# Double stores, VectorE and ScalarE programs without alignment, and a first load issued from ScalarE, in a batched matrix product on Trainium2

## Chip, cores, metric

One core of one Trainium2 chip. The metric is device microseconds of one execution; lower is better. Each kernel is run several times, and one execution has a profile. "Span" is the time from the first to the last instruction in the profile, which is some 1.8 us less than the device time of the same run.

## The reference

```python
# a: 16 x 512 (k) x 512 (m), b: 16 x 512 (n) x 512 (k), float32
def reference(a, b):
    return np.matmul(a.transpose(0, 2, 1), b.transpose(0, 2, 1)).astype(np.float32)
```

Per batch, 1 MB of a and 1 MB of b are read and 1 MB is written: 50.3 MB in all.

## The kernel before

Five engine programs run side by side, joined by semaphores. SyncE issues the loads and the last stores, ScalarE casts a to bf16, copies half of the result out of PSUM (where TensorE leaves its sums) and issues the other stores, VectorE casts b, moves the transposed b and copies the other half. TensorE transposes b and multiplies. The parts that matter here, with cuts marked:

```python
    LOADS = 4          # buffers of a and of b
    OUTS = 7           # result buffers, of one batch each
    LAG = 3
    FETCH = 128
    TAIL = 5           # stores issued by SyncE, at the end
    # ...
        def store(eng, j):
            eng.dma_start(out_v[j], o_sb[j % OUTS][:]).then_inc(
                o_out[j % OUTS] if j + OUTS < B else stored, 16
            )

        def run_sp(sp):
            for i in range(B):
                s, use = i % LOADS, i // LOADS
                if use:
                    sp.wait_ge(turned, i - LOADS + 1)
                sp.dma_start(b_sb[s][:], b_v[i]).then_inc(b_in[s], 16)
                if use:
                    sp.wait_ge(summed, MO * (i - LOADS) + 1)
                sp.dma_start(a_sb[s][:], a_v[i]).then_inc(a_in[s], 16)
            # ... the last five stores
    # ...
            dve.addr_align(FETCH, max_nops=0)      # head of VectorE's program
            cast_b(0)
            cast_b(1)
            turn(0)
            # ...
        def run_act(act):
            act.addr_align(FETCH, max_nops=0)      # head of ScalarE's program
            cast_a(act, 0, slice(None), 2)
            for i in range(B - 2):
                if i + 1 >= OUTS:
                    act.wait_ge(o_out[(i + 1) % OUTS], 16 * ((i + 1) // OUTS))
                cast_a(act, i + 1, slice(None), 2)
                copy_out(act, i, slice(2, 4), oa_go)
                if 0 <= i - LAG < B - TAIL:
                    store(act, i - LAG)
            # ...
```

Each `addr_align` leaves a branch in the trace, ScalarE's at 0.90 us (line 164) and VectorE's at 0.97 us (line 149).

## Time and profile before

| what | before |
|---|---|
| device time, median of 3 runs | 125.23 us (125.19 to 125.35) |
| span of the profiled run (it took 125.51 us) | 123.7 us |
| bytes moved, mean rate | 50.35 MB, 407 GB/s |
| busiest engine | TensorE, 69% of the span |
| two data queues together | 97.2% of 16 DMA engines' span |

The prediction shows and reads the lines for this. In short: DMA is full from the second slice to the last but one, no computing engine is, and the end waits for stores.

The prediction and all that follows use the packet records in the trace: start, duration, size and queue of each DMA packet. They carry no number of the DMA engine. I put them into 16 chains by time: in steady work each record starts 3 ns before the one ahead of it on its engine ends. Two chains of the same phase can be exchanged by this, so counts per chain are good to a few packets, while the ends of the 16 chains and the landings at the semaphores (16 for each transfer, 768 for the 48 transfers of the kernel before) are records themselves.

### The profile page before, as it was taken

Reading aid. Unit: us, or ns where it says so; the run is one execution under the profiler, and the core shown is the slowest. Engines: PE = TensorE matmul, PEld = TensorE weight load, DVE = VectorE, ACT = ScalarE, POOL = GpSimd, SP = SyncE. Lnnn points to the kernel's source line nnn. Section 1 sums busy time; section 2 is a strip of 40 time slices with the busy share of each in tenths; the row PEclk is TensorE's granted clock in tenths of the full one; section 3 lists DMA queues with packets and bytes.
Section 4 is the critical chain, followed back from the end, with each engine's and each line's share of the span. In section 5 each row is a group of like instructions: output and inputs, shape, how many; then the busy total and the mean of one; then the engine's idle time right before and its main releaser. Section 6 shows DMA issues by size and latency. Waiting matters only on the chain. (4 is left out here: it accounts for less than half of the span.)

```text
span 123.7 us, 1099 instructions
## 1 busy us (share of the span) xinstructions
PE 84.9 (69%) x392; PEld 48.2 (39%) x392; DVE 58.0 (47%) x50; ACT 45.9 (37%) x34; POOL 0.7 (1%) x6
## 2 busy tenths in 40 slices
PE   0042399949994997799499919919859965869600
PEld 0040155536462644455364602613535442524400
DVE  0032518455737755594653734716167370762200
ACT  0009410880466086317353080090906226034100
POOL 2000000000000000000000000000000000000000
PEclk9999999999999999999999995995899999599996
DMA  2999999999999999999999999999999999999992
GB/s 58 421 424 429 424 426 421 424 421 424 418 424 387 424 424 424 424 426 424 429 432 426 426 434 429 424 424 424 429 424 424 434 426 429 432 424 432 421 424 85
DMA packets 6914, 50.35 MB, mean 407 GB/s; under 512 B 768, under 2 KB 768, under 8 KB 768
## 3 DMA queue, kind: packets, MB, share of 16 engines
q1 hardware_dynamic: 5328, 38.80, 75.1%
q10 hardware_dynamic: 1584, 11.54, 22.1%
q14 instruction: 2, 0.02, 0.1%
HBM read 33.55 MB, written 16.78 MB: 407 GB/s over the span
## 5 line engine op out<-in xcount | busy, mean ns | idle before, releaser
L205 PE MATMUL o_ps<-bt_sb,a_bf 128*128 128x512 bf16 x256 | 67.5, 414 | 22.7 <-PEq L183 22.4
L205 PEld LDWEIGHTS o_ps<-bt_sb,a_bf 128*128 128x128 bf16 x256 | 28.5, 116 | 55.2 <-issue 33.8
L123 ACT CAST a_bf<-a_sb 128x2048 bf16<-128x2048 f32 (+1 forms) x16 | 29.6, 1847 | 33.8 <-DMA a_sb<-in_a_dram 33.8
L137 DVE CAST b_bf<-b_sb 128x2048 bf16<-128x2048 f32 x16 | 19.5, 1222 | 24.8 <-DMA b_sb<-in_b_dram 24.8
L132 DVE COPY o_sb<-o_ps 128x1024 f32<-128x1024 f32 (+1 forms) x17 | 19.7, 1160 | 20.3 <-PE o_ps L205 20.3
L193 PE MATMUL bt_ps<-identity,b_bf 128*128 128x128 f32 x136 | 21.0, 303 | 8.7 <-PEq L183 8.7
L132 ACT COPY o_sb<-o_ps 128x1024 f32<-128x1024 f32 (+1 forms) x17 | 16.3, 961 | 27.2 <-PE o_ps L205 27.2
L193 PEld LDWEIGHTS bt_ps<-identity,b_bf 128*128 128x128 f32 x136 | 20.3, 209 | 12.9 <-issue 10.9
L143 DVE COPY bt_sb<-bt_ps 128x1024 f32<-128x1024 f32 x16 | 19.5, 1221 | 11.6 <-PE bt_ps L193 11.6
L123 ACT ACT_TABLE_LOAD x1 | 1.3, 1283 | 9.1 <-DMA a_sb<-in_a_dram 9.1
L123 DVE CAST a_bf<-a_sb 128x1024 bf16<-128x1024 f32 x1 | 0.7, 694 | 0.5 <-DMA a_sb<-in_a_dram 0.5
L109 POOL TENSOR_SCALAR_AFFINE_SELECT identity<-identity 128x128 f32<-128x128 f32 x1 | 0.3, 292 | 0.2 <-POOL identity L107 0.2
L107 POOL MEMSET identity<- 128x128 f32 x1 | 0.2, 204 | 0.7 <-SPq L48 0.7
L249 POOL MEMSET const-bfloat16-1.0<- 128x1 bf16 x1 | 0.1, 101 | 0.0
L249 POOL MEMSET const-uint8-127<- 128x1 uint8 x1 | 0.1, 101 | 0.0
L249 POOL MEMSET const-float32-0.0<- 128x1 f32 x1 | 0.1, 98 | 0.2 <-issue 0.2
L249 POOL MEMSET const-float32-1.0<- 128x1 f32 x1 | 0.1, 98 | 0.0
## 6 DMA issues: line engine op xcount, KB each, us to landing
b_sb<-in_b_dram SPq DMA_DIRECT2D x16, 1024.0 KB, 16.5
a_sb<-in_a_dram SPq DMA_DIRECT2D x16, 1024.0 KB, 16.4
out_dram<-o_sb ACTq DMA_DIRECT2D x11, 1024.0 KB, 9.1
out_dram<-o_sb SPq DMA_DIRECT2D x5, 1024.0 KB, 8.4
```

The lines of the kernel that those rows point to most:

```text
L107: pool.memset(identity[:], 0.0).then_inc(id_go, 1)
L109: pool.affine_select(out=identity[:], in_=identity[:], compare_op=mybir.AluOpType.not_equal, fill=1.0, base=0, pattern=[[-1, P]], channel_ ...
L123: copy(a_bf[i % 2][:, part, :], a_sb[s][:, part, :]).then_inc(ac_go, n)
L132: copy(o_sb[i % OUTS][:, rm, :], o_ps[h][:, p, :]).then_inc(go, 1)
L137: dve.tensor_copy(b_bf[i % 2][:], b_sb[i % LOADS][:]).then_inc(bc_go, n)
L143: dve.tensor_copy(bt_sb[i % 2][:].rearrange("p j (ni no) -> p j ni no", no=NO), bt_ps[i % 2][:].rearrange("p j no ni -> p j ni no"),).then ...
L193: last = pe.transpose(bt_ps[x][:, j, no, :], w[:, no, j, :], identity[:])
L205: last = pe.matmul(o_ps[h][:, q, :], a_r[:, rk, 2 * h + q, :], bt_h[:, rk // 2, rk % 2, :], start=(rk == 0), stop=(rk == KO - 1),)
L249: nc = _bacc.Bacc("TRN2", target_bir_lowering=False, num_devices=1)
```

## The change

The intent: fewer transfers and fewer instructions on ScalarE, so that the programs of VectorE and ScalarE run without alignment and yet without an instruction packet in the span; and a start at which the first a is issued beside the first b.

```diff
-    OUTS = 7
+    OUTS = 5
     LAG = 3
-    FETCH = 128
-    TAIL = 5
+    TAIL = 3
+    H = B // 2
+    STORED = H - (H - OUTS) + 1
 ...
-        o_sb = [sb(f"o_sb{s}", [P, MO, N], f32) for s in range(OUTS)]
+        o_sb = [sb(f"o_sb{s}", [P, 2, MO, N], f32) for s in range(OUTS)]
 ...
-        def store(eng, j):
-            eng.dma_start(out_v[j], o_sb[j % OUTS][:]).then_inc(
-                o_out[j % OUTS] if j + OUTS < B else stored, 16
-            )
+        def store(eng, j, part=slice(0, 2)):
+            eng.dma_start(
+                out_v[2 * j + part.start:2 * j + part.stop].rearrange("b p mo n -> p b mo n"),
+                o_sb[j % OUTS][:, part],
+            ).then_inc(o_out[j % OUTS] if j + OUTS < H else stored, 16)
 ...   (SyncE)
-                sp.dma_start(a_sb[s][:], a_v[i]).then_inc(a_in[s], 16)
+                if i % 2 == 0 and i // 2 >= OUTS:
+                    sp.wait_ge(o_out[i // 2 % OUTS], 16 * (i // 2 // OUTS))
+                if i:
+                    sp.dma_start(a_sb[s][:], a_v[i]).then_inc(a_in[s], 16)
 ...   (SyncE's stores: two double ones, then batch 14 and batch 15 alone)
 ...   (VectorE: no alignment; its last two copies out as one; ScalarE's last two accordingly)
-            dve.addr_align(FETCH, max_nops=0)
-            copy_out(dve, B - 1, 0, last_go)
-            copy_out(dve, B - 1, 2, last_go)
+            copy_out(dve, B - 1, slice(0, 2), last_go)
 ...   (ScalarE: no alignment, no waits for result buffers, first load of a)
-            act.addr_align(FETCH, max_nops=0)
+            act.dma_start(a_sb[0][:], a_v[0]).then_inc(a_in[0], 16)
-                if i + 1 >= OUTS:
-                    act.wait_ge(o_out[(i + 1) % OUTS], 16 * ((i + 1) // OUTS))
-                if 0 <= i - LAG < B - TAIL:
-                    store(act, i - LAG)
+                j, odd = divmod(i - LAG, 2)
+                if odd and 0 <= j < H - TAIL:
+                    store(act, j)
```

More of the change, by code (lines that the diff above doesn't have):

```diff
@@ L92, in run_sp @@
                     sp.wait_ge(summed, MO * (i - LOADS) + 1)
-                sp.dma_start(a_sb[s][:], a_v[i]).then_inc(a_in[s], 16)
-            for j in range(B - TAIL, B):
-                if j + 1 < B:
-                    sp.wait_ge(summed, MO * (j + 1) + 3)
-                else:
-                    sp.wait_ge(last_go, MO)
-                store(sp, j)
-            sp.reg_mov(all_stored, 16 * OUTS)
+                if i % 2 == 0 and i // 2 >= OUTS:
+                    sp.wait_ge(o_out[i // 2 % OUTS], 16 * (i // 2 // OUTS))
+                if i:
+                    sp.dma_start(a_sb[s][:], a_v[i]).then_inc(a_in[s], 16)
+            for j in range(H - TAIL, H - 1):
+                sp.wait_ge(summed, MO * (2 * j + 2) + 3)
+                store(sp, j)
+            sp.wait_ge(summed, MO * (B - 1) + 3)
+            store(sp, H - 1, slice(0, 1))
+            sp.wait_ge(last_go, 3)
+            store(sp, H - 1, slice(1, 2))
+            sp.reg_mov(all_stored, 16 * STORED)
         def run_pool(pool):
@@ L131, in copy_out @@
             p = rm - 2 * h if isinstance(rm, int) else slice(None)
-            copy(o_sb[i % OUTS][:, rm, :], o_ps[h][:, p, :]).then_inc(go, 1)
+            copy(o_sb[i // 2 % OUTS][:, i % 2, rm, :], o_ps[h][:, p, :]).then_inc(go, 1)
         def run_dve(dve):
@@ L159, in run_dve @@
             cast_a(dve, B - 1, slice(KO // 2, KO), 1)
-            copy_out(dve, B - 1, 0, last_go)
-            copy_out(dve, B - 1, 2, last_go)
+            copy_out(dve, B - 1, slice(0, 2), last_go)
         def run_act(act):
-            act.addr_align(FETCH, max_nops=0)
+            act.dma_start(a_sb[0][:], a_v[0]).then_inc(a_in[0], 16)
             cast_a(act, 0, slice(None), 2)
             for i in range(B - 2):
-                if i + 1 >= OUTS:
-                    act.wait_ge(o_out[(i + 1) % OUTS], 16 * ((i + 1) // OUTS))
                 cast_a(act, i + 1, slice(None), 2)
                 copy_out(act, i, slice(2, 4), oa_go)
-                if 0 <= i - LAG < B - TAIL:
-                    store(act, i - LAG)
-            act.wait_ge(o_out[(B - 1) % OUTS], 16 * ((B - 1) // OUTS))
+                j, odd = divmod(i - LAG, 2)
+                if odd and 0 <= j < H - TAIL:
+                    store(act, j)
             cast_a(act, B - 1, slice(0, KO // 2), 1)
             copy_out(act, B - 2, slice(2, 4), oa_go)
-            copy_out(act, B - 1, 1, last_go)
+            copy_out(act, B - 1, 2, last_go)
             copy_out(act, B - 1, 3, last_go)
```

## The prediction

0.7 us for the instruction packets, 0.04 for semaphore packets and 0.05 for the first load make 0.8 (0.1 without the first), and at 0.7 to 0.3 that is 0.6 us.

> **What bounds the kernel now.** I looked first at the page's rows over time, then at its queues, then at sums over stretches of time, and last at what SyncE waits for at the end. On the page, DMA stands against every engine that computes:
>
> ```profile
> PE 84.9 (69%) x392; PEld 48.2 (39%) x392; DVE 58.0 (47%) x50; ACT 45.9 (37%) x34; POOL 0.7 (1%) x6
> ...
> DMA  2999999999999999999999999999999999999992
> GB/s 58 421 424 429 424 426 421 424 421 424 418 424 387 424 424 424 424 426 424 429 432 426 426 434 429 424 424 424 429 424 424 434 426 429 432 424 432 421 424 85
> ...
> q1 hardware_dynamic: 5328, 38.80, 75.1%
> q10 hardware_dynamic: 1584, 11.54, 22.1%
> q14 instruction: 2, 0.02, 0.1%
> ```
>
> No engine is busy over 69% of the span, while the DMA row is 9 from the second slice to the last but one, and the two data queues together took 75.1 + 22.1 = 97.2% of what 16 engines have. The windows (length, busy time by engine, clock, DMA share, GB/s) say the same by stage:
>
> ```profile
> 0.00:3.10 3.10, 0.00 (x0) 0.00 (x0) 0.00 (x0) 0.00 (x0) 0.70 (x6) 1.00 0.30 61
> 3.10:18.60 15.50, 6.18 (x21) 3.67 (x21) 4.20 (x4) 5.08 (x3) 0.00 (x0) 1.00 1.01 424
> 18.60:37.10 18.50, 16.67 (x85) 9.95 (x84) 11.27 (x10) 9.13 (x7) 0.00 (x0) 1.00 1.01 422
> 37.10:40.20 3.10, 1.39 (x8) 0.65 (x8) 2.36 (x2) 2.13 (x2) 0.00 (x0) 1.00 1.00 386
> 40.20:108.00 67.80, 53.66 (x250) 29.98 (x249) 36.84 (x31) 26.45 (x19) 0.00 (x0) 0.92 1.01 427
> 108.00:121.00 13.00, 6.99 (x36) 3.90 (x34) 3.30 (x4) 3.13 (x4) 0.00 (x0) 1.00 1.00 423
> ```
>
> Loads alone (3.1 to 37.1 us) run at 422 to 424 GB/s, loads mixed with stores at 427, stores alone (from 108 us) at 423. So the rate depends neither on direction nor on queue. TensorE is close to full only in 18.6 to 37.1 us (16.67 of 18.5 us) and still doesn't slow the DMA, as loads are queued ahead of it. The chain of waits on the page ends with PE at 116.4 us of 123.7, and is not the chain that matters; SyncE's own waits show that one (us in total, times, longest):
>
> ```profile
> SPq L260 <- DMA out_dram<-o_sb: 5.8, 1, 5.8
> ```
>
> SyncE sits 5.8 us at the end for stores that were all issued by 116.1 us. The bound is thus: start of the first transfer, plus bytes over a fixed rate, plus completion of the last.
>
> In the packet records this closes. There are 6,144 data packets of 8,192 bytes, 384 for each of 16 DMA engines; the usual record is 309 ns and the usual spacing from start to start 306 ns. 384 x 0.306 = 117.5 us. There are 768 four-byte packets (48 transfers x 16) of 9 ns, 48 an engine, which with the 3 ns overlap cost about 6 ns each, 0.3 us. The first data packet starts at 1.96 us, 1.0 us after SyncE began the first issue at 0.95; eight engines start by 2.04 us, the rest at 2.69 to 2.81, and first packets of up to 1.3 us make all reach their steady pace at about 3.1. A dip at 39.1 to 40.3 us, as the first store starts to move, costs about 0.3 us. The last packets then end at 120.97 to 121.49 us on fourteen engines, and at 121.97 and 122.21 on two. The last landing is at 122.68, the program's end at 123.7.
>
> [...]427 GB/s with both queues, 424 with one. [...]So a load of a on ScalarE's queue will share with the load of b rather than follow it. No first pair of loads in this trace shows that; stores do show it, as most 1 MB stores take 4.3 to 5.1 us from first to last packet beside loads, twice the 2.45 us a megabyte needs alone. [...]the trace has 9 ns records, so fewer transfers save little. [...]VectorE and ScalarE each take the branch that the alignment made, at 0.97 and 0.90 us, and two packets of q14 follow, at 1.93 us (1,356 ns) and 3.41 us (309 ns). Each has 8,192 bytes[...]. Whose they are the records don't say; I infer it from the times.
>
> **The change, part by part.**
>
> *Stores of two batches.* The bytes and the 8,192-byte pieces stay. ScalarE issues 5 stores, not 11, SyncE 4, not 5: 41 transfers instead of 48. Seven fewer semaphore packets an engine x 6 ns = 0.04 us saved. ScalarE saves 6 issues of 338 ns less the one it gains for a, some 1.7 us, and its waits for store buffers; all of that beside an engine 37% busy, so 0.
>
> *Could DMA run dry meanwhile?* The first store starts to be issued at 43.8 us, not 36.4. From the records, loads issued less data moved are lowest before the store, 2.1 MB (5 us of work) at 40 us; without the early store the same count gives 2.3 MB at 42.0, 2.1 at 45.0 and 1.85 at 48.6. The new wait is tighter: SyncE holds load a of batch 10 until the first double store has landed. Stores in this trace start to move some 3.5 us after the issue, so 47.5 us; 2 MB at half rate take 9.8 us; with landing some 57.9 us, against an issue at 51.4 now. By then 21 loads are issued, 22.1 MB moved, 2 of them stored: 0.9 MB left on SyncE's queue (2.1 us), while the second double store, issued at about 55.2, starts near 58.7. Close, not dry: 0. The later waits leave 2 MB and more. At the end six batches rather than five are issued from SyncE, the last load lands by my count near 105 rather than 110 us, and computing ends sooner, under stores that are queued anyway: 0.
>
> *Instruction blocks.* Without the alignment both engines run straight on; the built programs shrink from 74 to 67 instructions on ScalarE and from 64 to 62 on VectorE. [...]the two q14 packets go. Each displaced a data packet (309 ns) and upset the start of its DMA engine: a data record of 838 ns follows the second. Two packets and two late engines, 0.5 and 0.7 us behind the others: I take these for the same two. Then the last data packet ends at about 121.49 rather than 122.21: 0.7 us saved.
>
> *First load of a by ScalarE.* SyncE's second issue (starts 1.39 us, 0.43 us long) moves to ScalarE, free at about 0.9 to 1.0. DMA engines then already have 2.45 us of b to move, so an earlier a adds nothing; perhaps 0.05 us for an issue ahead of SyncE's. Interleaved, b lands near 9 us rather than 6.6. VectorE's first cast and PE's first transposes slip by up to 2.5 us, yet turning batch 0 waits behind the cast of b of batch 1 until 12.71 us even now, and 3 MB have moved by the same time either way. So the first product, at 14.4 us, should hardly move.
>
> Sum: 0.7 + 0.04 + 0.05 = 0.8 us if the fetches go, 0.1 if not. At 0.7 to 0.3 that is 0.6 us: 125.23 - 0.6 = 124.6.
>
> **The rivals.** *The fetch stays or moves*: [...]engines have slack and a packet costs a DMA engine 0.3 us, so the time stays at 125.1 or 125.2. *DMA runs dry at the new wait*: 0.9 MB is a thin margin and one slow stretch could cost 1 to 2 us, 125.5 to 126.5. Against it speaks that the store queue has 2 MB of its own at that time. *The start improves more*: two queues at once might bring the late eight engines (0.7 us behind) in at once; then 123.9. Against it: the early ones' first packets take so long that all are level at 3.1 us. *Fewer, larger stores move faster*: 427 GB/s mixed against 424 with loads alone leaves nothing to win, as packets have the same size.
>
> **Range and chances.** The middle is the weighted sum; 124.0 needs the fetch saving and a gain at the start, 125.5 a small loss at the new wait. 2% is 2.5 us: for a gain that long nothing is left between 97.2% and full, and a loss of that size takes a real stall. I give 1% to faster, 2% to slower.
>
> **What would show it right or wrong.** q14 gone from the queues, with both last engines ending within 0.6 us of the others, shows the fetch step right; q14 there with equal time, that it failed. A DMA row below 9, or GB/s under 380 near 55 to 62 us, shows the new wait to bite. First landings of a and b both near 9 us with PE's first product at 14.4 show the start right. The rate in stretches with stores should stay at 423 to 427 GB/s; over 430 would break the fixed-rate argument and with it the prediction.

## The result, and the profile after

The changed kernel took 125.43 us (median of 4 runs, 125.18 to 125.62), the kernel before 125.21 beside it (125.14 to 125.35). The ratio is 1.0015 with a 95% interval of 0.9992 to 1.0037. Neither the gain of 0.6 us came nor any other.

The page of the changed kernel, the rows over time and the queues:

```profile
DMA  3999999999999999999999999999999999999991
GB/s 72 395 432 435 430 424 419 424 416 419 422 416 419 424 424 424 424 435 432 427 432 424 427 424 424 424 424 432 424 435 427 424 432 429 430 424 422 424 424 69
...
q1 hardware_dynamic: 5296, 38.80, 74.9%
q10 hardware_dynamic: 1504, 11.53, 22.4%
```

DMA is as full as before, and the q14 line is gone: no instruction packet lies in the span. The same stretches as in the prediction (start:end, length, busy us of PE, PEld, DVE, ACT and POOL, clock, DMA share, GB/s):

```profile
3.10:18.60 15.50, 6.86 (x24) 4.35 (x25) 4.81 (x4) 5.08 (x3) 0.00 (x0) 1.00 1.00 422
18.60:37.10 18.50, 16.46 (x82) 9.46 (x80) 10.82 (x10) 9.56 (x8) 0.00 (x0) 1.00 1.01 422
37.10:40.20 3.10, 1.59 (x8) 0.84 (x9) 2.19 (x2) 1.70 (x1) 0.00 (x0) 1.00 1.01 418
40.20:108.00 67.80, 52.43 (x258) 29.98 (x256) 38.72 (x33) 27.04 (x20) 0.00 (x0) 0.97 1.01 426
108.00:121.00 13.00, 4.76 (x24) 2.86 (x24) 1.31 (x2) 2.52 (x4) 0.00 (x0) 0.89 1.01 427
```

The rates are those of before within 1%, except that the dip at 37 to 40 us (386 GB/s before) is absent. SyncE's waits:

```profile
SPq L98 <- DMA out_dram<-o_sb: 26.1, 3, 8.9
...
SPq L260 <- DMA out_dram<-o_sb: 8.5, 1, 8.5
```

The new wait for result buffers (L98) takes 26.1 us of SyncE in three waits, and DMA stays full through all of them. SyncE now waits 8.5 us for the end, as computing ends sooner, with the last stores queued longer. The start, from the timeline of the changed kernel (start, duration, instruction):

```profile
0.91 0.40 ACTq L168 DMA_DIRECT2D a_sb<-in_a_dram  x1
0.95 0.86 SPq L93 DMA_DIRECT2D b_sb<-in_b_dram  x2
1.86 0.42 SPq L100 DMA_DIRECT2D a_sb<-in_a_dram  x1
...
8.63 1.23 DVE L144 CAST b_bf<-b_sb 128x2048 bf16<-128x2048 f32 x1 [8.63 <-DMA b_sb<-in_b_dram]
...
13.69 3.58 PE L205 MATMUL o_ps<-bt_sb,a_bf 128*128 128x512 bf16 x8 [1.74 <-PEq L183]
```

In the timeline of the kernel before the same places read:

```profile
1.86 1.55 SPq L90 DMA_DIRECT2D b_sb<-in_b_dram  x1
...
6.60 1.23 DVE L137 CAST b_bf<-b_sb 128x2048 bf16<-128x2048 f32 x1 [6.60 <-DMA b_sb<-in_b_dram]
...
14.38 3.58 PE L205 MATMUL o_ps<-bt_sb,a_bf 128*128 128x512 bf16 x8 [4.45 <-PEq L183]
```

The first b comes 2.0 us later, since it shares with a, and the first product still starts 0.7 us earlier. SyncE's third issue took 1.55 us beside the instruction packet of before and takes 0.42 now.

Where then is the gain? The end of each of the 16 chains of packets, in us, shows it:

```
before   120.97 121.00 121.06 121.07 121.18 121.35 121.37 121.41 121.43 121.44 121.44 121.45 121.49 121.49 121.97 122.21
changed  120.92 120.93 120.97 120.97 120.98 120.99 121.00 121.01 121.02 121.18 121.19 121.21 121.24 121.26 121.26 122.08
```

Of the two late chains one is gone. Fifteen DMA engines are done by 121.26 us, a quarter of a microsecond sooner than the fourteen of before, and one still works until 122.08. (The missing dip would explain that quarter: 32 GB/s less over 3.1 us at 418 GB/s is 0.24 us, an estimate from the two windows that no run tests; e3, with slow packets near 46 us, has its fifteen done by 121.15.) In the windows, DMA share of 16 engines just before the end, before and then changed:

```profile
121.50:121.95 0.45, 0.00 (x0) 0.00 (x0) 0.00 (x0) 0.00 (x0) 0.00 (x0) 0.66 0.13 55
```

```profile
121.30:122.05 0.75, 0.00 (x0) 0.00 (x0) 0.00 (x0) 0.00 (x0) 0.00 (x0) 0.50 0.05 22
```

0.13 is two of 16 engines, 0.05 is one. The last engine decides: the last data packet moved by 0.12 us only (one profile of each kernel, and the spans of one kernel's runs differ by up to 0.5 us), the last landing from 122.68 to 122.55. The second part of the answer is not in the span at all: device time less span was 1.98 to 2.09 us in the four runs of the changed kernel, and is 1.73 to 1.83 in the 31 runs of the kernel before that were made beside the experiments. Together with the control c1 below, the mean span is 123.34 us over 9 runs of the changed kernel and 123.54 over those 31: 0.19 us gained in it, 0.25 lost outside.

### The profile page after: what moved, and what is told of

Its sections match the earlier page's. It is cut to its first block, busy times and chain, and to the rows that moved or that the text cites. A ratio compares the mean times of both kernels' runs of the same rounds, so it can differ in the third digit from the quotient of the medians.

```text
span 123.6 us, 1091 instructions
## 1 busy us (share of the span) xinstructions
PE 82.1 (66%) x392; PEld 47.5 (38%) x392; DVE 57.9 (47%) x49; ACT 45.9 (37%) x34; POOL 0.7 (1%) x6
## 5 line engine op out<-in xcount | busy, mean ns | idle before, releaser
L205 PE MATMUL o_ps<-bt_sb,a_bf 128*128 128x512 bf16 x256 | 65.1, 403 | 20.1 <-PEq L183 19.8
L139 DVE COPY o_sb<-o_ps 128x1024 f32<-128x1024 f32 x16 | 19.6, 1224 | 20.9 <-PE o_ps L205 20.8
L193 PEld LDWEIGHTS bt_ps<-identity,b_bf 128*128 128x128 f32 x136 | 19.8, 208 | 14.9 <-issue 13.0
## 6 DMA issues: line engine op xcount, KB each, us to landing
out_dram<-o_sb SPq DMA_DIRECT2D x2, 2048.0 KB, 13.3
```

Source lines behind the costliest of these rows:

```text
L139: copy(o_sb[i // 2 % OUTS][:, i % 2, rm, :], o_ps[h][:, p, :]).then_inc(go, 1)
L193: last = pe.transpose(bt_ps[x][:, j, no, :], w[:, no, j, :], identity[:])
L205: last = pe.matmul(o_ps[h][:, q, :], a_r[:, rk, 2 * h + q, :], bt_h[:, rk // 2, rk % 2, :], start=(rk == 0), stop=(rk == KO - 1),)
```

## The experiments

The theory after the result, called B below: in every kernel one DMA engine takes on average 2 to 6 ns more for a packet than the others once loads and stores mix (c1: 311.7 and 313.9 ns against 309.0), and ends last; the instruction packets made two others late as well, which mattered less. The rival, A: the prediction's, that the engines with the instruction packets alone make the end late. Kernels of one set ran on one chip with the kernel before: e1 to e4 on one, c1 and e5 to e7 on a second, e7b and e8 to e10 on a third. Every kernel computed the correct result.

### e1: the kernel before without alignment

```diff
-            dve.addr_align(FETCH, max_nops=0)
-            act.addr_align(FETCH, max_nops=0)
```

> The kernel before without the alignment of the VectorE and ScalarE programs, nothing else changed. Theory A (the two instruction packets make two DMA engines late, and those engines end the program): the packets are gone from the span, the last data packet ends near 121.5 us, the time falls 0.5 to 0.7 us under the kernel before. Theory B (one DMA engine whose packets average 311 to 313 ns where the others need 309 ends last anyway): the packets are gone and the first load's landings lie within 0.4 us of each other instead of 1.0, but by the end one engine is again 0.9 us behind; the time stays within 0.2 us of before. Rival C[...]: an instruction packet appears later in the span, and the time stays within 0.2 us.

Measured: 125.64 us (125.62 to 125.67) against 125.30, ratio 1.003 (1.0017 to 1.0043), so no gain but a small loss. No instruction packet lies at the start. The landings of the first load lie within 0.33 us of each other, where in the kernel before two were 0.46 and 0.91 us behind the eighth. Yet at the last store one landing is 0.95 us behind the eighth, and fourteen of the chains end by 121.41, the fifteenth at 121.52, the last at 122.01 us. The windows of e1 show one engine at work near the end:

```profile
121.55:122.00 0.45, 0.00 (x0) 0.00 (x0) 0.00 (x0) 0.00 (x0) 0.00 (x0) 0.50 0.04 18
```

Theory A falls, B fits. Rival C is right too: an instruction packet of 309 ns comes at 113.7 us instead. It isn't what makes the last engine late, as the last landing of the transfer before it, near 112 us, is 0.77 us behind the eighth already. Nor does the loss lie there: the mean span is 123.56 us against 123.50, and 0.30 us of the loss is outside it (2.08 against 1.79). It is there in e4 as well (112.3 us) and in no profile with double stores; e1 and e4 are the two whose ScalarE program has the eleven single stores and no alignment. So it is with double stores that no such late instruction packet lies in the span; that their fewer instructions are the reason was the author's estimate. That part of the intent came true.

### e2: the changed kernel with alignment

```diff
+            dve.addr_align(128, max_nops=0)
             cast_b(0)
 ...
+            act.addr_align(128, max_nops=0)
             act.dma_start(a_sb[0][:], a_v[0]).then_inc(a_in[0], 16)
```

> The changed kernel with the alignment put back, also ahead of ScalarE's first load of a. Theory A: two instruction packets come back and the time rises by 0.5 us or more over the changed kernel (about 126). Theory B: the packets come back and two engines land the first loads 0.5 to 0.9 us late; the end is set by the latest of these and the slow engine, so within 0.3 us of the changed kernel (125.2 to 125.7), unless the slow engine is one of the two, then up to 0.9 us more.

Measured: 125.94 us (125.68 to 126.54), ratio 1.0066 (1.005 to 1.0082). Two instruction packets are back (1.97 and 3.43 us), two engines land the first load 0.48 and 0.93 us late. That is A's figure, but something that neither theory foresaw came with it: ScalarE's load comes behind its branch, and its issue takes 2.94 us where it took 0.40. From the timeline of e2:

```profile
1.34 2.94 ACTq L170 DMA_DIRECT2D a_sb<-in_a_dram  x1
...
13.54 1.28 ACT L130 ACT_TABLE_LOAD   x1 [13.54 <-DMA a_sb<-in_a_dram]
...
17.02 0.59 PE L207 MATMUL o_ps<-bt_sb,a_bf 128*128 128x512 bf16 x1 [7.09 <-PEq L185]
```

The first a lands at 13.3 us, behind two megabytes of SyncE's loads and beside a third, and the first product starts at 17.0 us, 3.3 later than in the changed kernel. Five chains end by 121.35 us, the other eleven between 121.54 and 122.50, with the eighth at 121.87, so here most engines are late: packets take 350 to 750 ns in stretches near 49, 64 and 72 us. The rates of 47 to 50.4, 62 to 65.4 and 70 to 73.4 us are 412, 405 and 383 GB/s in e2, 405, 395 and 388 in e10, and 424, 424 and 422 in the kernel before: some 0.6 us of work in each, an estimate, and as much as the loss (0.64 and 0.58 us in the medians). That the late load brings these stretches about is not shown. As a test of A this run is spoilt; e10 repeats what spoilt it.

### e3: the changed kernel with the first a from SyncE

```diff
-                if i:
-                    sp.dma_start(a_sb[s][:], a_v[i]).then_inc(a_in[s], 16)
+                sp.dma_start(a_sb[s][:], a_v[i]).then_inc(a_in[s], 16)
 ...
-            act.dma_start(a_sb[0][:], a_v[0]).then_inc(a_in[0], 16)
```

> The changed kernel with the first load of a given back to SyncE. If the start is hidden, as predicted: same time within 0.15 us, b lands near 5.7 us and a near 8.1 us, first product at 14 us or a little before. If the two queues at the start cost or save something: first data packets or the last one move by more than 0.2 us, and the time with them.

Measured: 125.27 us (124.95 to 125.29), ratio 0.9991 (0.9978 to 1.0004). b lands at 5.7, a at 8.1 us, the first product starts at 13.47. The start is hidden as predicted: with b three microseconds sooner the first product moves by 0.2. The last data packet ends at 121.85, again alone, with fifteen engines done by 121.15. Time less span is 1.90 us instead of 2.04.

### e4: the changed start with single stores

The kernel before without alignment (as e1), and with the first a from ScalarE:

```diff
+            act.dma_start(a_sb[0][:], a_v[0]).then_inc(a_in[0], 16)
             cast_a(act, 0, slice(None), 2)
 ...
-                sp.dma_start(a_sb[s][:], a_v[i]).then_inc(a_in[s], 16)
+                if i:
+                    sp.dma_start(a_sb[s][:], a_v[i]).then_inc(a_in[s], 16)
```

> The changed kernel's start (no alignment, first load of a by ScalarE) with the single stores and seven buffers of the kernel before. Theory B: one engine ends 0.8 to 1.2 us behind the rest as in the changed kernel, time 125.0 to 125.5. Rival D (double stores cost what the missing fetches save): time 124.5 to 124.8, and the last data packet near 121.4 us.

Measured: 125.52 us (125.24 to 125.79), ratio 1.0018 (1.0004 to 1.0032). One engine ends alone at 122.19, the others by 121.69. Its instruction packet at 112.3 us makes it not quite free of fetches, and its last engine is later than that of the changed kernel, not sooner. Double stores neither cost nor bring anything in DMA time that these runs can tell: rival D falls.

### c1: the changed kernel again

> The changed kernel itself, as the control of this set. If what its first profile showed holds: no instruction packet in the span and one just after its end; one DMA engine whose data packets average 311 us/1000 or more in the second half and whose last landing comes 0.7 to 1.2 us after the others; time minus span about 2.0 us against 1.8 for the kernel before; ratio to before 1.000 to 1.003.

Measured: 125.41 us (125.21 to 125.46) against 125.41 for the kernel before, ratio 0.9995 (0.9982 to 1.0009). No instruction packet in the span, one just after it (124.4 us). Chains: fifteen by 121.33, the last at 121.93. Its landing at the last store is 0.92 us behind the eighth, and at the two stores before that 0.90 and 0.91: it is not the tail of the last transfer. In the stretch from 72 to 82 us one chain's data packets average 311.7 ns, the others 309.0; from 100 to 110 us it is 313.9 against 309.0. The kernel before shows the same picture: from 60 to 70 us 312.7 ns in one chain and at most 309.8 in the others. With loads alone it doesn't show: from 30 to 36 us all chains of the kernel before and of the changed one average 312 to 316 ns. Time less span: 2.03 against 1.78. So this pair of medians gives a plain account: span 123.4 against 123.6, 0.2 us gained in it, 0.25 lost outside.

### e5: one DMA engine with eight packets less

The last store in two parts, of 120 and 8 partitions. The page of the run counts 663 packets under 512 bytes, where c1's has 656 for its 41 transfers of 16 each. 663 is 40 x 16 + 15 + 8, which fits 120 partitions on 15 engines and 8 on eight. The count that SyncE waits for rises by one transfer (not shown).

```diff
-            store(sp, H - 1, slice(1, 2))
+            for lo, hi in ((0, 120), (120, 128)):
+                sp.dma_start(
+                    out_v[B - 1, lo:hi], o_sb[(H - 1) % OUTS][lo:hi, 1]
+                ).then_inc(stored, 16)
```

> The changed kernel with the last store split into partitions 0 to 119 and 120 to 127, so that one of the 16 DMA engines has 8 packets less and eight of them one more. If the slow engine ends the program and is the one spared: the last data packet ends at 121.5 to 121.7 instead of 122.1 us, time 0.3 to 0.6 us under the control. If the slow engine sets the end but is another: unchanged, or 0.3 us later if it got the extra packet. If the late end is no property of an engine (rival: the last transfer's own tail), one landing is again 0.8 to 1.2 us after the rest whatever is spared.

Measured: 125.75 us (125.52 to 125.96), ratio 1.003, 0.34 us over c1. The packet records agree with that count: one chain ends at 119.27 us without any packet of the last store, and its packets averaged 309.0 ns, so the one spared was not the slow one. Another was last with the store of batch 14, at 119.44 us, and ended last at 122.21. 119.44 + 9 x 0.306 = 122.20: it had nine packets, so it is one of the eight that got one more. The last packet came 0.27 us later than in c1 and the time 0.34. That is the case "another engine, with the extra packet", and it fits B. It isn't clean: that the last chain is the slow engine is inferred, as chains can be exchanged, and other chains were slowed too (packets of the 120-partition part took up to 569 ns, those of the 8-partition part up to 351, and the fifteenth chain ends at 121.93).

### e6, e7, e7b: one of the two programs aligned

Both with the first a on SyncE (as e3). e6 has `dve.addr_align(128, max_nops=0)` ahead of `cast_b(0)`, e7 and its repetition e7b have `act.addr_align(128, max_nops=0)` as ScalarE's first instruction.

> The changed kernel with the first load of a on SyncE (as e3) and the alignment ahead of VectorE's program alone. If each aligned engine fetches one block at its start and each unaligned one may fetch at its end: exactly one instruction packet near 1.9 us, one DMA engine late from the first load by 0.5 or 0.9 us. Time minus span falls from e3's 1.9 to 1.8 us if VectorE's end made the late fetch, and stays if ScalarE's did. Time within 0.3 us of e3 (125.3), as the slow engine ends 0.9 us behind anyway, unless the fetch falls on it.

> The same with the alignment ahead of ScalarE's program alone. One instruction packet near 1.9 us; time minus span falls to 1.8 us if ScalarE's end made the late fetch, and stays at 1.9 if VectorE's did. Exactly one of e6 and e7 should keep the packet after the end, if one engine alone made it; both lose it only if it belongs to neither. Time within 0.3 us of e3.

> Control: the changed kernel with the first load of a on SyncE and the alignment ahead of ScalarE alone, again. If its lead was real: ratio to before 0.996 to 1.000, time minus span 1.9 us. If it was chance, a ratio up to 1.001. One engine's landings again 0.5 to 1.0 us behind at the end.

| run | device time, us | ratio to before | instruction packet at the start | one after the end | late chains, us |
|---|---|---|---|---|---|
| e6 | 125.30 | 1.0000 (0.9986 to 1.0014) | 3.38 us, 802 ns | yes | 121.92, 122.14 (the other 14 by 121.40) |
| e7 | 125.22 | 0.9984 (0.9970 to 0.9998) | 1.95 us, 1,422 ns | no | 121.73, 121.80 (the other 14 by 121.58) |
| e7b | 125.29 | 0.9996 (0.9984 to 1.0008) | 1.94 us, 1,422 ns | no | 121.71, 121.73 (the other 14 by 121.25) |

Each aligned program makes one instruction packet at the start, and each packet makes one DMA engine late from the first load on (1.08, 0.64 and 0.83 us behind the eighth landing). Over the profiles without another disturbance the count is clear: no packet at the start, one late chain (changed, c1, e1, e3, e4); one packet, two late chains (e6, e7, e7b, and e9 below), though in e7 the two are only 0.15 and 0.21 us behind the next. Only the kernel before doesn't fit: two packets, but two late chains and not three. Its last chain ends on packets of 315 and 314 ns, so the slow engine seems to be one of its two; which of its late starts was made up for on the way, perhaps in the dip at 39 us, isn't settled. In the window of e7b two engines are at work:

```profile
121.30:121.70 0.40, 0.00 (x0) 0.00 (x0) 0.00 (x0) 0.00 (x0) 0.00 (x0) 0.50 0.10 41
```

The engine with the packet and the slow one end within 0.25 us of each other, so taking the packet away leaves the time nearly as it is. The lead of e7 was not repeated by e7b. The packet after the end belongs to ScalarE's program, as it goes when ScalarE is aligned; but it doesn't cost the time outside the span, since e6 has it with 1.79 us and e7 hasn't with 1.91.

### e8: one packet less for half of the engines

e7 with the store of batch 14 in four parts, of 112, 7, 7 and 2 partitions, to take a packet from nine engines. The page of the run counts 672 packets under 512 bytes against 656 in e7, which is 40 x 16 + 16 + 7 + 7 + 2: this fits parts that went to 16, seven, seven and two engines. If the two are among the seven, nine engines get 7 packets of this batch rather than 8, five get 9 and two get 10.

```diff
-            store(sp, H - 1, slice(0, 1))
+            for lo, hi in ((0, 112), (112, 119), (119, 126), (126, 128)):
+                sp.dma_start(
+                    out_v[B - 2, lo:hi], o_sb[(H - 1) % OUTS][lo:hi, 0]
+                ).then_inc(stored, 16)
```

> The control with the store of batch 14 split into partitions 0 to 111, 112 to 118, 119 to 125 and 126 to 127[...]. If the slow engine is the eighth: its last packet comes 0.3 us earlier, and the end is shared with the first two engines, 0.1 to 0.3 us under the control. If it is one of the first seven: 0.3 us later, 0.6 if it is one of the first two. If the late end is no matter of packets per engine: no change, or a loss from three more transfers.

"The eighth" is to be read as one of the nine with a packet less, "the first seven" as the other seven and "the first two" as the two with ten packets.

Measured: 126.15 us (125.83 to 127.03), ratio 1.0079, 0.85 us over e7b. The end can't tell which engine is slow: the few-partition transfers themselves were slow, with packets of up to 1,300 and 974 ns, and four chains end at 122.43 to 122.84 us. The windows of e8 from 119 us:

```profile
119.00:120.00 1.00, 0.00 (x0) 0.00 (x0) 0.00 (x0) 0.00 (x0) 0.00 (x0) 0.50 0.94 385
120.00:121.00 1.00, 0.00 (x0) 0.00 (x0) 0.00 (x0) 0.00 (x0) 0.00 (x0) 0.50 0.78 328
121.00:122.00 1.00, 0.00 (x0) 0.00 (x0) 0.00 (x0) 0.00 (x0) 0.00 (x0) 0.50 0.29 123
```

Nine engines, those with a packet less, have ended by 120.89 us. This way of relieving one engine costs more than its lateness. The packets before that do tell something. When the store of batch 13 ends, two chains are late, at 116.98 and 117.10 us, and the other fourteen are done by 116.30: the slow engine and the one with the instruction packet, if B is right. By the packets that follow between their semaphore writes, which are records of four bytes (7, 1, 1 and 1 in the one, 7, 1 and 1 in the other, then 8), the one got ten packets of batch 14 and the other nine. Then the slow engine is not one of the nine with a packet less.

### e9, e10: the changed kernel with one program aligned

The changed kernel as it is, with VectorE (e9) or ScalarE (e10) aligned alone, in the latter ahead of its load.

> The changed kernel as it is, with the alignment ahead of VectorE alone. Time minus span, which was 2.03 us in the changed kernel, 1.9 with a on SyncE and 1.79 with VectorE aligned as well: 1.79 if VectorE's place alone makes it, 1.92 if the two add up, 2.03 if only ScalarE's program matters. Late instruction packet after the end present, as ScalarE stays unaligned. Time 125.1 to 125.5.

> The changed kernel with the alignment ahead of ScalarE alone, and so ahead of its load of a. Time minus span: 1.9 us if the late packet of ScalarE's program cost the difference to e3, 2.03 if it did not. The load of a is then issued [...]at 3 us or later, and queues behind SyncE's loads: if e2 was slow for that, b of batch 0 lands near 5.7 and a at 10 us or later, the first product comes at 15 us or later, and the time is 125.6 or more; if e2 was slow for other reasons, 125.2 to 125.5.

e9: 125.30 us, ratio 1.0004 (0.9991 to 1.0018). e10: 125.87 us (125.68 to 127.21), ratio 1.0078: the load's issue takes 2.96 us, the first product starts at 16.9 us, and ten chains are late (121.58 to 122.56 us, the other six are done by 121.06), much as in e2. The prediction for e2's cause held there as far as the late load goes, and the slow stretches near 49, 64 and 72 us are the same. The mean of device time less span over each kernel's runs:

| VectorE aligned | ScalarE aligned | first a from | kernel | time less span, us |
|---|---|---|---|---|
| yes | yes | SyncE | before, three chips | 1.78 to 1.79 |
| yes | yes | ScalarE | e2 | 1.78 |
| yes | no | SyncE | e6 | 1.79 |
| no | yes | SyncE | e7, e7b | 1.91 |
| no | yes | ScalarE | e10 | 1.89 |
| no | no | SyncE | e3 | 1.90 |
| yes | no | ScalarE | e9 | 1.90 |
| no | no | ScalarE | changed, c1 | 2.04, 2.03 |

Two steps of 0.11 to 0.14 us add up: VectorE without alignment is one, a first load at the very head of an unaligned ScalarE program is the other. (e1 with single stores has 2.08, and e4's runs scatter from 1.73 to 2.19, so the place of the program matters beyond these two.) What happens in that time the trace doesn't show.

## Why the prediction was wrong

**The bound** was right: a start, bytes at a fixed rate, a last landing. DMA share and GB/s are the same in every stretch.

**Double stores** were right: 427 GB/s with stores alone (the stretch of 423 that the prediction takes for that still held the end of the last load, which landed at 110.2 us), no gain from larger transfers, and 0.04 us for fewer semaphore packets is below what these runs resolve.

**The new wait** was right: load a of batch 10, expected at 57.9 us, was issued at 57.1, and no slice of the DMA row but the first and the last is below 9. The last load landed near 107.3 rather than my 105, which nothing depended on.

**The start** was right: both first loads land at 8.4 to 8.6 us, the first product isn't later. That it is 0.7 us earlier comes from the missing instruction packet, not from ScalarE's load: without a packet it starts at 13.47 to 13.85 us (the changed kernel, c1, e1, e3, e4, e5), with one or two at 14.09 to 14.59 (the kernel before, e6, e7, e7b, e8, e9), e2 and e10 with their late load left out.

**The instruction blocks** are the step that failed. It said: "Two packets and two late engines, 0.5 and 0.7 us behind the others: I take these for the same two. Then the last data packet ends at about 121.49 rather than 122.21: 0.7 us saved." That the packets go and that they make engines late was right; e6, e7 and e1 show it. That one is ScalarE's and one VectorE's, which it inferred, e6 and e7 show too. (Of the eight early starts that it counts at 2.04 us one is the first of these packets.) That no other engine would be late was wrong. In place of 0.72 us the last packet moved by 0.12 us (first profile) and 0.27 (c1), because one more DMA engine, slower by some nanoseconds a packet in the second half, ends 0.5 to 0.8 us after the rest. In the changed kernel its landing is 0.24 us behind the eighth at 45 us and 1.19 at the end: 0.95 us lost in 76, or 3.8 ns for each of 248 packets, which agrees with the means by chain. e1, which takes away the alignment and nothing else, ended at 122.01 with that chain late, and the time did not fall. The sign was there beforehand: the trace of the kernel before has this slow chain too. I had taken the usual record of all engines together, 309 ns, and not a mean for each.

**The second miss** was not in the sum: 0.25 us more outside the span, which no view of the profile shows, cancels what the span gained. It appeared with the alignment's removal and ScalarE's early load, and how it arises stays open.

**The rivals** "the start improves more" and "DMA runs dry" did not happen, and "the fetch stays" did not either. That the result, 125.43, lies between the times of the last two (125.1 to 125.2, and 125.5 or more) is luck. So what would vanish was named rightly; its term in the sum was too large by a factor of 3 to 6, and a cost that wasn't looked for took back the rest.

Open: which DMA engine is slow and why (by e8 one of the seven that got more packets there, if the late chains are what B says); why packets of all engines slow down for a microsecond or so near the first store in most profiles (a slice of 360 to 409 GB/s there, against some 425), and three times in e2 and e10; what the 0.25 us outside the span are; why the kernel before has two late chains and not three. None of the versions tried beats the kernel before beyond its noise: e3 and e7b are equal to it, and e7's lead was not repeated.

## What to carry to other kernels

Where DMA is full from end to end, as here, the time is the end of the slowest of 16 DMA engines (here 122.08 us against 121.26 for the other fifteen): look at the ends and the mean packet time of each engine, not at the average, before crediting the removal of a delay on some of them. A delay that goes is worth only its distance to the next latest (here 0.12 us of the 0.72 forecast). And compare device times as well as spans: what a change costs before the first or after the last instruction doesn't show in the profile (here 1.78 to 2.08 us, in the mean of a kernel's runs).
